# First layer's attention: full-row scores with a doubled low part of k, v split per head, and reloads issued by GpSimd

## The chip, the core and the metric

The kernel runs on one core of one Trainium2 chip. The metric is the device time of one execution in microseconds; the time given for a kernel is the median of its runs. Stretches of the profile are given in microseconds from the start of the span.

## The reference

Two layers over 1024 positions of width 1024, in float32. Layer 0 mixes with differential attention (mixer A, 4 heads) and causal pooling (mixer B); layer 1 mixes with banded attention (mixer C). Each layer ends with a gated MLP of inner width 2816 that has a width-3 causal convolution. Cut to what matters here:

```python
def diff_attention(q, k, v, lam, lam_init, sub_g):      # per head: two 64-wide maps m = 0, 1
    s = jnp.einsum('bqhmd,bkhmd->bhmqk', q, k) * scale + bias   # causal, ALiBi
    p = jax.nn.softmax(s, axis=-1)
    attn = p[:, :, 0] - lam * p[:, :, 1]
    return jnp.einsum('bhqk,bkhe->bqhe', attn, v)       # v is 128 wide per head

def conv_glu_ffn(x, norm_g, w_up, conv_w, conv_b, w_down):
    h = rms_norm(x, norm_g) @ w_up                      # 1024 -> 2 * 2816
    c = causal_conv3(h) ; gate, up = split(c)
    return x + (silu(gate) * up) @ w_down               # 2816 -> 1024
```

## The kernel before

All matrix products take float32 operands as a high and a low part (`split`: ScalarE copies the high part, VectorE or GpSimd subtracts it to get the low part; lines 125 to 128). A product of two such operands is three matmuls. The program is written with a tile framework whose scheduler orders each engine's instructions; `weave` interleaves in program order a main generator (the attention of one head) with a side generator (projections that are needed later), at a rate of side cost per main cost. Tiles come from pools of a fixed number of buffers; a new tile takes a buffer that is free, or the next one that becomes free.

The stages, by the profile: setup and pools of layer 0 (to about 100 us), projection of q, k and v of mixer A and the attention of its four heads with the output projection (about 100 to 445 us), the up half of the MLP (to about 895 us), the down half (to about 1130 us), then the same for layer 1 with mixer C.

**Scores of mixer A.** Per head, `stack_q` transposes q on TensorE and builds for each map m a tile of 128 rows: 64 rows with the high part of q, the other 64 with its low part. `stack_k` builds for each map a tile `hi` that holds the high part of k in both halves of the rows, and the low part of k. With one `lo` tile (`len(los) == 1`), map 0 has its low part in rows 0 to 63 and map 1 in rows 64 to 127 of the same tile. `scores` then issues two matmuls into one PSUM bank: line 623 over all 128 rows (q high and q low against k high), and line 624 over the 64 rows of map m (q high against k low). Mixer C calls the same functions with two `lo` tiles: line 616 copies each low part to the other 64 rows, and line 624 runs over 128 rows there.

For query block j (128 queries, j = 0 to 7) the keys come in chunks of up to 512 columns; a chunk of 128 is widened to 256. VectorE adds the bias table and takes the minimum (line 694), ScalarE exponentiates (698), VectorE combines the two maps (711), TensorE transposes the result (718), `split` (127, 128), and line 729 multiplies with v.

**v of mixer A.** `project_v` leaves v of two heads in two raw tiles (`va`, `vb`). `split_v` makes four tiles, two blocks of keys and two heads in each, once for heads 0 and 1 and once for heads 2 and 3. These tiles, q, k and others share the tag `g` with 9 buffers in this stage (`MIX_A`).

**Side work.** For heads 0 to 2 the side generator is `dense` (line 553, matmuls of 256 columns into bank `psd`); from late in head 2 it is `project_out` (line 119, into `psd`).

**The down half** (`ffn_down`). For each pair of row blocks i, `fetch` reloads the gated activations from DRAM (`gd`, into tag `gr`, 4 buffers, or `xg` for the first pair) and loads the weights (`wr`, 2 buffers); both are split. The residual x is reloaded from DRAM (line 533, 8 tiles). All these are issued by SyncE (SP), each queue in order. `contract` adds each product to x (line 268). GpSimd issues no DMA; its work is `split` subtractions (line 128) and one-column memsets (837, `claim`).

Of the kernel before, what the change touches and what calls it, by code (L numbers as in the profile page):

```python
# [14 lines left out]
F32R = mybir.dt.float32r  # L15
# [5 lines left out]
P = 128  # L21
# [43 lines left out]
class Trunk:  # L65
# [445 lines left out]
    def ffn_down(self, layer, xs, gd, after, begin=lambda: None):  # L511
        nc, I = self.nc, self.I

        def fetch(i):
            ws, gs = [], []
            for k in range(2):
                for lst, tag, stage, src in (
                        (gs, "g", "gr", gd[(i + k) * P:(i + k + 1) * P, :]),
                        (ws, "ws", "wr", I["w_down"][layer, i + k])):
                    if i == 0 and lst is gs:  # L520
                        tag = stage = "xg"
                    raw = self.big(stage)
                    nc.sync.dma_start(raw[:], src)
                    hi, lo = self.big(tag, F32R), self.big(tag, F32R)
                    with self.urgent():
                        self.split(raw[:], hi[:], lo[:])
                    lst.append((hi, lo))
            return ws, gs

        nxt = fetch(0)  # L530
        x = [self.big("x") for _ in range(ND)]
        for d in range(ND):
            nc.sync.dma_start(x[d][:], xs[d * P:(d + 1) * P, :])
        for i in range(0, NF - 2, 2):
            ws, gs = nxt
            nxt = fetch(i + 2)
            self.drain(self.contract(ws, [self.halves(g) for g in gs], x, banks="dqsdqsqs"))
        ws, gs = nxt
        begin()
        return lambda h: self.contract(ws, [self.halves(g) for g in gs], x, after, "qd", (h,))  # L540
# [107 lines left out]
                    raws[b // 4][:, (b % 4) * 256:(b % 4 + 1) * 256], po, AF.Copy, scale=r[:, b:b + 1])  # L648
            yield 2.6

    def split_v(self, raws):
        vs = []
        for i in range(4):
            v = self.big("g", F32R, (P, 2, 2, 2, P))
            src = raws[i // 2][:, (i % 2) * 512:(i % 2 + 1) * 512].rearrange("p (b h e) -> p b h e", b=2, h=2)
            for b in range(2):
                hi, lo = v[:, b, :, 0, :], v[:, b, :, 1, :]
                self.split(src[:, b], hi, lo)
            vs.append(v)
        return vs  # L660

    def a_attend(self, h, raws, vs, o, before, tails):
# [1 line left out]
        tab = self.big("t")  # L664
        nc.sync.dma_start(tab[:], I["tab_a"][h])
        q = [self.big("g", F32R) for _ in range(2)]
        k = ([self.big("g", F32R) for _ in range(2)], [self.big("g", F32R) for _ in range(1)])
        get = lambda o: (lambda b: raws[b // 4][:, (b % 4) * 256 + o:(b % 4) * 256 + o + P])
        self.stack_q(get(0), self.gq[:, 0:1], q)
        self.stack_k(get(P), self.par[:, PAR_AK:PAR_AK + 1], *k)  # L670
# [3 lines left out]
        for j in range(NB):  # L674
# [47 lines left out]
            for c, w, pt in pts:  # L722
                th, tl = self.half(F32R), self.half(F32R)
                self.split(pt[:, :w], th[:, :w], tl[:, :w])
                for kb in range(w // P):
                    b = c // P + kb
                    v = vs[b // 2][:, b % 2, h % 2].rearrange("p t e -> p (t e)")
                    for t, tt in enumerate((th, tl)):
                        nc.tensor.matmul(po[:, :256], tt[:, kb * P:(kb + 1) * P], v,  # L729
                                         start=(b == 0 and t == 0), stop=(b == j and t == 1))  # L730
# [134 lines left out]
    def layer_a(self, w, norm, bd, after):  # L865
# [55 lines left out]
                yield from self.contract(ws, [self.halves(m) for m in ms], x, banks="d")  # L921

        side, out_side = dense(), project_out()
        vs = self.split_v(va)
        mixes = [self.big("x") for _ in range(AH - 1)] + [self.big("rbc")]
        self.claim(mixes[0])
        for h in range(AH):
            if h < AH - 2:
                self.claim(mixes[h + 1])
            if h == 2:  # L930
                vs = self.split_v(vb)
            def before(h=h):
                if h > 0:
                    tails[h - 1]()
# [340 lines left out]
```

## Time and profile before

| | before |
|---|---|
| median of 3 runs | 2176.08 us (2173.35 to 2179.15) |
| profiled execution, its own time | 2179.32 us |
| its span | 2177.5 us |
| TensorE (PE) busy | 2103.5 us, 97% |
| VectorE (DVE) busy | 1648.1 us, 76% |
| ScalarE (ACT) busy | 1010.7 us, 46% |
| GpSimd (POOL) busy | 129.2 us, 6% |
| chain that ended last: share of PE | 89% |

The busy time of PE runs from a matmul's start to its modelled end, so that pipelined matmuls overlap in it: what a matmul takes from the stream is read as the distance from its start to the start of the next one.

### The profile page before, as it was taken

The page shows a single profiled execution, that of the slowest core. Times are in us where ns is not written, and L with a number is a line of the kernel's source. Part 1 is how long each engine was busy: PE and PEld are TensorE (multiplying, and loading weights), DVE is VectorE, ACT ScalarE, POOL GpSimd, SP SyncE. Part 2 cuts the span into 40 slices and gives each one's busy share as a digit, 9 for nine tenths or more (in the row PEclk, how much of TensorE's full clock was granted, in tenths as well). Part 3 has the DMA queues.
Part 4 walks back from the last instruction along what each step waited for, and adds up shares of the span by engine and source line. Part 5 has one row for each costly group of instructions (what it writes and reads, how often), then busy time and mean ns, then how long its engine had stood idle before and what let it go on. Part 6 is the DMA issues. An engine that isn't in the chain of part 4 may idle for free.

```text
span 2177.5 us, 28523 instructions
## 1 busy us (share of the span) xinstructions
PE 2103.5 (97%) x10704; PEld 1768.6 (81%) x10704; DVE 1648.1 (76%) x3015; ACT 1010.7 (46%) x1887; POOL 129.2 (6%) x88
## 2 busy tenths in 40 slices
PE   8999999989999999899999999898999999989999
PEld 7988867767888888788889998787788888878887
DVE  6676787788777878667677887787877878776665
ACT  5465555336455455312144886654645555531210
POOL 1210132000000000000002020200000000000000
PEclk9999989989999999999999999999999999999999
DMA  4210122212222122622232011221222122262222
GB/s 166 88 40 30 59 88 68 78 39 97 77 88 87 70 86 87 243 78 98 76 107 79 30 40 49 68 78 58 97 78 82 74 87 78 97 227 92 82 93 78
DMA packets 59610, 186.02 MB, mean 85 GB/s; under 512 B 6864, under 2 KB 7376, under 8 KB 59472
## 3 DMA queue, kind: packets, MB, share of 16 engines
q1 hardware_dynamic: 52560, 171.62, 22.7%
q10 hardware_dynamic: 6912, 12.59, 1.5%
q8 instruction: 84, 1.38, 0.3%
q14 instruction: 54, 0.44, 0.1%
HBM read 142.23 MB, written 41.94 MB: 85 GB/s over the span
## 4 chain that ended last, share of the span: by engine, by line
PE 89%; DVE 7%; ACT 2%; issue 1%; DMA 0%; SPq 0%; ACTq 0%; DVEq 0%
PE pss L336 22%; PE psd L119 12%; PE psq L336 12%; PE psq L119 11%; PE pss L119 8%; PE psd L553 6%; PE psd L336 5%; PE pss L553 4%; PE pss L624 2%; PE psq L729 2%; PE pss L623 1%; PE pss L778 1%; PE psq L778 1%; DVE x L305 1%; PE psq L1023 1%
## 5 line engine op out<-in xcount | busy, mean ns | idle before, releaser
L336 PE MATMUL pss<-xg,ws 128*128 128x512 f32 x1248 | 297.6, 391 | 9.1 <-DVE xg L128 5.5
L336 PEld LDWEIGHTS pss<-xg,ws 128*128 128x128 f32 x1248 | 234.9, 189 | 60.4 <-DVE xg L128 6.3
L336 PE MATMUL pss<-T,ws 128*128 128x512 f32 x912 | 225.4, 390 | 3.4 <-ACT ws L127 3.4
L119 PE MATMUL psq<-g,ws 128*128 128x512 f32 x852 | 220.0, 392 | 5.8 <-ACT g L127 3.4
L336 PEld LDWEIGHTS pss<-T,ws 128*128 128x128 f32 x912 | 171.9, 189 | 40.0 <-ACT ws L127 4.3
L119 PEld LDWEIGHTS psq<-g,ws 128*128 128x128 f32 x852 | 160.4, 189 | 39.9 <-ACT g L127 3.9
L553 PE MATMUL psd<-ws,xg 128*128 128x256 f32 x1344 | 188.9, 287 | 0.5 <-DVE hms L562 0.5
L119 PE MATMUL psd<-xg,ws 128*128 128x512 f32 x624 | 171.5, 414 | 15.2 <-DVE x L268 13.1
L127 ACT ACTIVATE ws<-wr 128x512 fp32r<-128x512 f32 (+1 forms) x176 | 145.3, 829 | 78.5 <-PE pss L119 38.3
L553 PEld LDWEIGHTS psd<-ws,xg 128*128 128x128 f32 x1344 | 170.1, 191 | 7.5 <-issue 4.1
L119 PE MATMUL pss<-g,ws 128*128 128x512 f32 x684 | 176.1, 391 | 0.0
L127 ACT ACTIVATE g<-gr 128x1024 fp32r<-128x1024 f32 x40 | 41.6, 1051 | 289.4 <-PE pss L119 289.4
L336 PE MATMUL psq<-xg,ws 128*128 128x512 f32 x696 | 169.3, 391 | 0.0
L128 DVE TENSOR_TENSOR ws<-hf,ws 128x512 fp32r<-128x512 f32 x152 | 104.0, 688 | 69.0 <-ACT ws L127 68.9
L336 PEld LDWEIGHTS psq<-xg,ws 128*128 128x128 f32 x696 | 131.4, 189 | 27.5
L268 DVE TENSOR_TENSOR x<-psq,x 128x512 f32<-128x512 f32 x160 | 109.9, 688 | 55.9 <-PE psq L119 55.5
L119 PEld LDWEIGHTS pss<-g,ws 128*128 128x128 f32 x684 | 129.4, 189 | 27.1
L119 PEld LDWEIGHTS psd<-xg,ws 128*128 128x128 f32 x624 | 116.5, 196 | 42.7 <-DVE x L268 14.9
L128 POOL TENSOR_TENSOR ws<-wr,ws 128x1024 fp32r<-128x1024 f32 x38 | 94.2, 2487 | 950.9 <-ACT ws L127 912.4
L268 DVE TENSOR_TENSOR x<-psd,x 128x512 f32<-128x512 f32 x160 | 109.9, 688 | 50.7 <-PE psd L119 48.4
L128 DVE TENSOR_TENSOR ws<-wr,ws 128x512 fp32r<-128x512 f32 (+1 forms) x138 | 119.3, 866 | 20.6 <-ACT ws L127 20.6
L119 PE MATMUL psd<-g,ws 128*128 128x512 f32 x528 | 134.0, 389 | 0.0
(212 smaller groups left out, 3791.2 us busy)
## 6 DMA issues: line engine op xcount, KB each, us to landing
wr<-in_dram SPq DMA_DIRECT2D x130, 512.0 KB, 3.7
gd<-x SPq DMA_DIRECT2D x40, 512.0 KB, 2.6
gr<-gd SPq DMA_DIRECT2D x40, 512.0 KB, 4.5
x<-in_dram SPq DMA_DIRECT2D x38, 512.0 KB, 4.4
xd<-x ACTq DMA_DIRECT2D x48, 256.0 KB, 2.3
x<-in_dram SPq DMA_DIRECT2D x32, 256.0 KB, 3.5
x<-xd SPq DMA_DIRECT2D x16, 512.0 KB, 6.0
t<-in_dram SPq DMA_DIRECT2D x10, 512.0 KB, 3.6
```

The costliest lines, as they stand in the source:

```text
L119: self.nc.tensor.matmul(out, a, b, start=(k == 0), stop=(k == n - 1))
L127: nc.scalar.activation(hi, raw, AF.Copy)
L128: (eng or nc.vector).tensor_tensor(out=lo, in0=raw, in1=hi.bitcast(F32), op=ALU.subtract)
L268: nc.vector.tensor_tensor(out=xs, in0=po[:], in1=xs, op=ALU.add)
L305: nc.vector.scalar_tensor_tensor(out=xs, in0=xs, scalar=g, in1=self.nrbc[:, sl], op0=ALU.mult, op1=ALU.mult)
L336: nc.tensor.matmul(bank[:], a, b, start=start and k == 0, stop=k == n - 1, skip_group_check=open)
L553: self.nc.tensor.matmul(out, a, m[:, d % 4, :], start=(n == 0), stop=(n == 23))
L623: nc.tensor.matmul(out, q[:, qs], his[m][:, ks], start=True, stop=False)
L624: nc.tensor.matmul(out, q[rows, qs], lo[rows, ks], start=False, stop=True)
L729: nc.tensor.matmul(po[:, :256], tt[:, kb * P:(kb + 1) * P], v, start=(b == 0 and t == 0), stop=(b == j and t == 1))
L778: nc.tensor.matmul(pu[:], a, b, start=d + n == 0, stop=d == ND - 1 and n == 2)
L1023: nc.tensor.transpose(pt[:, (2 * kb + t) * P:(2 * kb + t + 1) * P], pv[:, 2 * kv + t, k0 + kb * P:k0 + (kb + 1) * P], self.idn[:])
```

## The change

Three edits. The low part of k gets two tiles in mixer A, so that `stack_k` copies each low part to the other 64 rows (line 616, four ScalarE copies of 64x512 per head) and `scores` runs line 624 over 128 rows. `split_v` now makes the two tiles of one head, and is called at the start of each head. In the down half, the reloads of `gd` and of x are issued by GpSimd instead of SyncE; the weights stay with SyncE.

```diff
@@ ffn_down
-                    nc.sync.dma_start(raw[:], src)
+                    (nc.gpsimd if lst is gs else nc.sync).dma_start(raw[:], src)
...
-            nc.sync.dma_start(x[d][:], xs[d * P:(d + 1) * P, :])
+            nc.gpsimd.dma_start(x[d][:], xs[d * P:(d + 1) * P, :])
@@ split_v
-    def split_v(self, raws):
+    def split_v(self, raws, h):
         vs = []
-        for i in range(4):
-            v = self.big("g", F32R, (P, 2, 2, 2, P))
-            src = raws[i // 2][:, (i % 2) * 512:(i % 2 + 1) * 512].rearrange("p (b h e) -> p b h e", b=2, h=2)
-            for b in range(2):
-                hi, lo = v[:, b, :, 0, :], v[:, b, :, 1, :]
-                self.split(src[:, b], hi, lo)
+        for i in range(2):
+            v = self.big("g", F32R, (P, 4, 2, P))
+            src = raws[i][:].rearrange("p (b h e) -> p b h e", b=4, h=2)[:, :, h, :]
+            self.split(src, v[:, :, 0, :], v[:, :, 1, :])
             vs.append(v)
@@ a_attend
-        k = ([self.big("g", F32R) for _ in range(2)], [self.big("g", F32R) for _ in range(1)])
+        k = ([self.big("g", F32R) for _ in range(2)], [self.big("g", F32R) for _ in range(2)])
...
-                    v = vs[b // 2][:, b % 2, h % 2].rearrange("p t e -> p (t e)")
+                    v = vs[b // 4][:, b % 4].rearrange("p t e -> p (t e)")
@@ layer_a
-        vs = self.split_v(va)
...
-            if h == 2:
-                vs = self.split_v(vb)
+            vs = self.split_v((va, vb)[h // 2], h % 2)
```

What moves on the engines, at the two places of which the prediction speaks (lines of the changed kernel after `split_v` are two or three lower: 696 is 698 of before, 716 is 718, 727 is 729, 732 is 734).

ScalarE at the start of head 0, before: lines 609 and 610 write the high part of k, 560 and 561 evict the side work's bank, 698 exponentiates.

```order
L609 ACTIVATE g_1170<-psq_1190,par 64x512
L610 ACTIVATE g_1170<-psq_1190,par 64x512
L560 ACTIVATE x_1224<-psd_1257 128x256
L561 ACTIVATE psd_1257<-psd_1257 128x256
L609 ACTIVATE g_1169<-psq_1201,par 64x512
L610 ACTIVATE g_1169<-psq_1201,par 64x512
L698 ACTIVATE t_1316,l_1315<-t_1316,mn_1320 128x128
L609 ACTIVATE g_1170<-psq_1201,par 64x512
L610 ACTIVATE g_1170<-psq_1201,par 64x512
```

The same place in the changed kernel:

```order
L609 ACTIVATE g_1155<-psq_1190,par 64x512
L610 ACTIVATE g_1155<-psq_1190,par 64x512
L127 ACTIVATE g_2041<-x_929 128x4x128
L616 ACTIVATE g_1158<-g_1158 64x512
L560 ACTIVATE x_1215<-psd_1276 128x256
L561 ACTIVATE psd_1276<-psd_1276 128x256
L616 ACTIVATE g_1157<-g_1157 64x512
L609 ACTIVATE g_1156<-psq_1190,par 64x512
L610 ACTIVATE g_1156<-psq_1190,par 64x512
L696 ACTIVATE t_1307,l_1306<-t_1307,mn_1311 128x128
```

The copies of the low part (616) stand between the high parts and the evictions of the side work, and the first half of head 1's v (`g_2041`) is split already here.

SyncE at the head of layer 0's down half, before (`wr` weights, `gr` and `xg` gated activations, `x` the residual, 357 a store of the up half):

```order
L357 DMA gd_72<-x_8081 128x1024
L523 DMA wr_8407<-in_dram 128x1024
L523 DMA gr_8249<-gd_72 128x1024
L533 DMA x_8233<-xd_69 128x1024
L533 DMA x_8234<-xd_69 128x1024
L533 DMA x_8235<-xd_69 128x1024
L533 DMA x_8236<-xd_69 128x1024
L523 DMA gr_8261<-gd_72 128x1024
L523 DMA gr_8401<-gd_72 128x1024
L523 DMA gr_8413<-gd_72 128x1024
L523 DMA wr_8419<-in_dram 128x1024
L533 DMA x_8237<-xd_69 128x1024
```

GpSimd at that place in the changed kernel:

```order
L523 DMA gr_8253<-gd_72 128x1024
L533 DMA x_8237<-xd_69 128x1024
L533 DMA x_8238<-xd_69 128x1024
L533 DMA x_8239<-xd_69 128x1024
L533 DMA x_8240<-xd_69 128x1024
L523 DMA gr_8265<-gd_72 128x1024
L523 DMA gr_8405<-gd_72 128x1024
L523 DMA gr_8417<-gd_72 128x1024
L533 DMA x_8241<-xd_69 128x1024
L533 DMA x_8242<-xd_69 128x1024
L523 DMA gr_8557<-gd_72 128x1024
L533 DMA x_8243<-xd_69 128x1024
```

The reloads keep their order among themselves and leave the weights' queue; they stand alone on GpSimd, the eighth tile of x as the sixteenth of the row that begins with `gr_8253`.

## Rows read from the trace of the kernel before

**Rows 1.** The page, part 1: engine, busy us, share, instructions.

```profile
PE 2103.5 (97%) x10704; PEld 1768.6 (81%) x10704; DVE 1648.1 (76%) x3015; ACT 1010.7 (46%) x1887; POOL 129.2 (6%) x88
```

**Rows 2.** Windows: stretch and length; busy us of PE, PEld, DVE, ACT, POOL; clock; DMA.

```profile
260.00:300.00 40.00, 37.86 (x179) 27.11 (x177) 34.28 (x95) 29.59 (x69) 18.00 (x12) 0.83 0.36 119
360.00:380.00 20.00, 19.20 (x85) 12.61 (x84) 18.15 (x48) 12.15 (x30) 10.35 (x5) 1.00 0.42 132
140.00:450.00 310.00, 297.01 (x1685) 239.40 (x1685) 242.08 (x649) 160.68 (x367) 47.78 (x30) 0.97 0.20 65
```

**Rows 3.** Chain in order of time (start, us, what): matmuls of 512 columns.

```profile
540.52 2.72 PE pss L336 x12
```

**Rows 4.** Timeline of PE, two places in mixer A (start, us, engine, line, operation).

```profile
165.72 0.39 PE L623 MATMUL pss<-g,g 128*128 128x512 f32 x1
166.04 0.49 PE L624 MATMUL pss<-g,g 64*128 64x512 f32 x1
166.46 0.50 PE L623 MATMUL pss<-g,g 128*128 128x512 f32 x1
166.89 0.50 PE L624 MATMUL pss<-g,g 64*128 64x512 f32 x1
167.32 0.86 PE L553 MATMUL psd<-ws,xg 128*128 128x256 f32 x5
...
210.34 0.36 PE L623 MATMUL pss<-g,g 128*128 128x256 f32 x1
210.63 0.38 PE L624 MATMUL pss<-g,g 64*128 64x256 f32 x1
210.94 0.74 PE L553 MATMUL psd<-ws,xg 128*128 128x256 f32 x4
```

**Rows 5.** Timeline of PE in mixer C, where line 624 has 128 rows.

```profile
1207.49 0.28 PE L624 MATMUL pss<-g,g 128*128 128x256 f32 x1
1207.60 0.28 PE L623 MATMUL pss<-g,g 128*128 128x256 f32 x1
1207.72 0.28 PE L624 MATMUL pss<-g,g 128*128 128x256 f32 x1
```

**Rows 6.** Groups by line and form: count, busy us, mean ns, idle before.

```profile
L624 PE MATMUL pss<-g,g 64*128 64x512 f32 x48 | 24.6, 512 | 0.0
L624 PE MATMUL pss<-g,g 64*128 64x256 f32 x32 | 11.9, 381 | 2.3 <-DVE g L612 2.3
L624 PE MATMUL pss<-g,g 64*128 64x384 f32 x16 | 7.0, 438 | 0.0
```

**Rows 7.** Windows of line 624 alone: PE and PEld busy us (and count).

```profile
260.00:300.00 40.00, 8.91 (x18) 3.70 (x18) 0.83 0.36 119
360.00:380.00 20.00, 5.26 (x13) 2.19 (x12) 1.00 0.42 132
```

**Rows 8.** Line 616 in mixer C: ns min/median/max, first and last start, form.

```profile
L616 ACT ACTIVATE g<-g x4: 617/631/635, 1195.8 to 1203.2; 64x512 fp32r<-64x512 f32 x4
```

**Rows 9.** Timeline of GpSimd and VectorE at 190 us.

```profile
190.35 2.39 POOL L128 TENSOR_TENSOR ws<-wr,ws 128x1024 fp32r<-128x1024 f32 x1
190.50 2.26 DVE L165 TENSOR_TENSOR nt<-nt,zh 128x4 f32<-128x4 f32 x1
```

**Rows 10.** Timeline at the head of layer 0's down half: SyncE, VectorE, PE.

```profile
890.28 2.68 SPq L533 DMA_DIRECT2D x<-xd  x4
...
904.38 0.69 DVE L268 TENSOR_TENSOR x<-psd,x 128x512 f32<-128x512 f32 x1
...
905.12 2.93 PE L119 MATMUL psd<-xg,ws 128*128 128x512 f32 x6 [5.71 <-DVE x L268]
...
925.30 1.29 DVE L268 TENSOR_TENSOR x<-psq,x 128x512 f32<-128x512 f32 x2 [0.66 <-PE psq L119]
```

**Rows 11.** The page, part 6: count, KB each, us from issue to landing.

```profile
x<-xd SPq DMA_DIRECT2D x16, 512.0 KB, 6.0
```

**Rows 12.** Windows: the loop of layer 0's down half.

```profile
950.00:1100.00 150.00, 150.00 (x663) 124.24 (x662) 103.89 (x138) 27.36 (x28) 0.00 (x0) 1.00 0.25 81
```

## The prediction, on record before the run

> **What bounds the kernel now.** I read the page first: PE is busy for 97% of the span and is most of the chain that ended last [rows 1]. So time goes only where PE's stream gets shorter, or where PE waits. Then the windows: over mixer A's attention, 140 to 450 us, PE is busy 297.0 of 310 us, DVE 242.1, ACT 160.7 [rows 2]. Two stretches in it are unlike the rest: at 260 to 300 and at 360 to 380 us DVE is busy 34.3 of 40 and 18.2 of 20 us and PE is not full. Outside them DVE is busy 242.1 - 34.3 - 18.2 = 189.6 of 250 us, 76%, and PE has next to no gaps. There the PE stream is the bound; in the two stretches the chain through DVE is. Last the timeline of PE, by starts: a busy time overlaps the next one, a start does not.
>
> **Scores: what a 64-row matmul takes from the stream.** A matmul of 512 columns in a plain run starts every 2.72/12 = 0.227 us [rows 3]; one of 256 columns, full rows, every 0.11 to 0.12 us, and this holds for lines 623 and 624 themselves in mixer C [rows 5]. In mixer A the same pair is far slower [rows 4]: from 165.72 the starts are 0.32 and 0.42 us apart, then 0.43 and 0.43, so a pair of 512 takes 0.74 to 0.86 us, 0.80 in the mean, where two plain ones take 0.45; the pair of 256 takes 0.29 + 0.31 = 0.60 where 0.24 would do. So each change between 128 and 64 rows costs some 0.1 to 0.2 us, on the matmul ahead of it and on the 64-row one. The excess is 0.35 us at 512, 0.36 at 256, and I take 0.36 at 384. With the counts [rows 6] that is 48 x 0.35 + 32 x 0.36 + 16 x 0.36 = 34 us of PE's stream. All of it goes, since the changed kernel has mixer C's form here. If the short kind of pair (0.74) were the rule, it would be 48 x 0.29 + 48 x 0.36 = 31.
>
> The Trainium skill (TensorE: Matmul & The Clock Gate, section "Why this matters for your kernels") points the other way: a single matmul on few rows takes as long as one on 128, and a gain comes only from several running at once. By that rule the 64-row matmul was never dear and the change gives PE nothing. The trace disagrees for matmuls in a mixed stream: 0.42 us against 0.227.
>
> **How much of the 34 us shortens the run.** Of the 96 pairs 18 + 13 = 31 lie in the two stretches that DVE bounds [rows 7], 11 us of the excess; 65 lie where PE bounds, 23 us. Where PE bounds, DVE goes from 189.6 of 250 to 189.6 of 227 us, 84%, so it does not become the bound on the whole, but PE's order is fixed, and an attention matmul that comes sooner finds its DVE result less often ready. The gain there lies between 23 and, if half is lost to such waits, 11 us; I take three quarters, 17, since DVE still has room. In the two stretches it lies between 11 and 0; I take a quarter, 3, nearer to 0, since PE there waits anyway. The clock was granted at 0.83 in the first of them, so part of that stretch ran at the lower level; I count nothing for it.
>
> **What the scores edit adds.** Sixteen ScalarE copies (line 616) at 0.63 us [rows 8], 10 us on an engine that is half idle: nothing by themselves. But they lengthen the way to a head's first scores by one or two copies, 0.6 to 1.3 us, and ScalarE waits in them for DVE's subtraction (line 612); queued behind them are the evictions 560 and 561, for which the side matmuls wait. In the changed order some 24 side matmuls stand between the first line 623 and line 624 of head 0 (none before) and 22 in head 1 (4 before): 24 x 0.12 = 2.9 us of cover. Bare, four heads would pay 2.4 to 5.2 us; covered, nothing; I take 1. By the same order the attention falls back against its side work by up to some 25 matmuls in heads 0 to 2, so the side work ends sooner against the heads that follow; I take 2 us for that, between 0 and 25 x 0.12 = 3.
>
> **v per head.** Half as many splits over the same elements: no gain counted. A head holds 8 of the 9 `g` buffers, and the second low tile of k of the next head takes the buffer of the last head's first v tile, so it waits for that head's last product. Between a head's last scores and the next head's first stand some 140 side matmuls in the first case, before and after, 17 us: nothing. Without that cover it would be one more chain of transposes and copies at three boundaries.
>
> **Reloads by GpSimd.** Sixty issues leave SyncE. In the loop PE is busy 150.00 of 150 us [rows 12], so a sooner or later reload changes nothing there. Only the heads of the two passes have something to win or lose: PE idles 5.71 us before 905.12, released by a DVE add at 904.38 [rows 10]. The x tiles for it were issued from 890.28 and land 6.0 us later in the median [rows 11], at 896.3, 8.1 us ahead of the add. So the add waited its turn on DVE, behind convolutions, and moving the loads cannot bring it forward. The order on DVE stays but for one gate product (1.2 us) ahead of four adds; between 0 and 1.2 us a pass, and I take 0, since PE drains a bank in 6 x 0.227 = 1.36 us and DVE adds in 0.6. No row shows a DMA issued by GpSimd. Its time on GpSimd is bounded by SyncE's 2.68/4 = 0.67 us [rows 10] and by GpSimd's own pass over 128x1024, 2.39 us [rows 9]; I take a value near the lower, as an issue does not walk the elements. Sixteen reloads from `gr_8253` to the eighth x tile pass in order; that tile is wanted at 925.30, so there is no loss up to (925.3 - 6.0 - 890.3)/16 = 1.8 us each. I take 0.
>
> **Sum.** -17 - 3 + 1 + 2 + 0 = -17 us. The profiled run, 2179.3 us (its span 2177.5 and 1.8 around it), would become 2162; it lies 3.2 us above the median of 2176.1, to which the same step gives 2159.
>
> **The rivals.** *All of it counts:* the 34 us go and DVE keeps pace. For it speaks that DVE's 242 us fit into 276; against it the two stretches near DVE's limit. 2176 - 34 + 0 to 3 = 2142 to 2145.
>
> *DVE takes over:* the waits grow by what PE saves. For it speaks that DVE is over 85% busy in 60 of the 310 us, and that GpSimd holds it up: a four-column operation took 2.26 us while GpSimd ran its pass at 190.35 [rows 9]. Against it, the 76% elsewhere. Loss of three quarters of the 23 us and of all the 11, with 3 paid: 2176 - 6 + 3 = 2173, so 2169 to 2177. Here belongs also that full rows bring nothing, because the slow pairs were waiting for something else: 2176 + 1 to 3 = 2177 to 2179, at 0.03; the rows speak against it, since plain and mixed pairs differ in a stream that waits for nothing. This is what the page cited above would have.
>
> *The reloads come late:* each reload holds GpSimd longer than 1.8 us, its queue is in order, and at the head of each down pass the DVE adds, with PE behind them, wait for the last x tiles. At 2.39 us the eighth tile lands (16 x 2.39) - (16 x 1.8) = 9 us late, 19 in two passes, and cancels the gain: 2178. At 3 us it is 16 x 1.2 = 19 a pass: 2159 + 38 = 2197. It decides from about 2.5 us. For it speaks that GpSimd and DVE hold each other up [rows 9] and that DVE is packed at that place; against it that a plain issue on SyncE takes a third.
>
> The Trainium skill (SBUF — State Buffer, section "SBUF: two separate sides") warns of this: a DMA that GpSimd issues has its descriptors written by GpSimd, which is locked out while DVE runs an operation that uses both ports for one tensor. No run here shows it so far; the operations of DVE in the down half take two tensors, so I leave the chance low.
>
> **How the numbers follow.** The forecast, 2151 to 2167: 0.58. All of it counts: 0.13. DVE takes over, full rows for nothing included: 0.18. Late reloads, 2170 to 2200: 0.11. For 8 in 10 the range takes the forecast, the upper part of the first rival and most of the second: 2144 to 2175. About 0.3%, 6.5 us, is what a measurement of this kernel can tell from no change: faster is below 2169.6, slower above 2182.6. Faster: 0.58 + 0.13 + 0.05 of the second rival + 0.01 of the third = 0.77; slower: 0.07 of the third; the same: 0.16.
>
> **What would show it.** In the profile after: starts 0.227 apart at lines 623 and 624 with 512 columns and 0.12 with 256; 140 to 450 us shorter by some 17 us, with DVE's share up and PE's waits on line 694's and 128's results up; idle time of PE at the heads of the down passes again near 5.7 us; GpSimd's issues under 1.8 us. It is wrong if the attention ends no sooner though the starts are close (DVE took over), if the starts stay apart (the rows were not the cause), or if PE's idle time before line 119 grows.

## The result, and the profile after

The changed kernel takes 2164.69 us in the median of 4 runs (2162.63 to 2166.92), the kernel before 2177.61 us in the runs beside them: a ratio of 0.9944, 95% interval 0.9931 to 0.9958, so by this ratio 12.2 us or 0.56% faster (the medians lie 12.9 us apart). The forecast was 2159 with a range of 2144 to 2175. The sign, the place and the mechanism of the gain were right; the gain is 12 us where 17 were forecast, and two errors of opposite sign stand behind that small difference. Of all the executions of the runs below one, of e6_zero_first, took 3455.18 us at a mean granted clock of 0.556; its ratio leaves it out.

In the page's part 1 of the changed kernel, PE is 31 us less busy than in [rows 1], ScalarE 8 us more (the copies), GpSimd 32 us more (the reloads' issues):

```profile
PE 2072.1 (96%) x10704; PEld 1768.5 (82%) x10704; DVE 1644.9 (76%) x3007; ACT 1019.0 (47%) x1895; POOL 161.0 (7%) x148
```

The pairs of the scores have the plain distance now. Timeline of PE in mixer A (start, us, engine, line, operation), to be held against [rows 4]:

```profile
206.34 0.39 PE L623 MATMUL pss<-g,g 128*128 128x512 f32 x1
206.57 0.40 PE L624 MATMUL pss<-g,g 128*128 128x512 f32 x1
206.81 2.18 PE L553 MATMUL psd<-ws,xg 128*128 128x256 f32 x17
...
211.39 0.28 PE L623 MATMUL pss<-g,g 128*128 128x256 f32 x1
211.51 0.28 PE L624 MATMUL pss<-g,g 128*128 128x256 f32 x1
211.63 0.64 PE L553 MATMUL psd<-ws,xg 128*128 128x256 f32 x4
```

From 206.34 the starts are 0.23 and 0.24 us apart, where 0.32 to 0.43 stood before; at 256 columns 0.12 and 0.12, as in mixer C [rows 5]. The last product with v starts at 414.6 us instead of 427.6, the first matmul of the MLP at 433.8 instead of 445.8, 12.0 us sooner. (The two profiled executions lie 15.9 us apart. Most of the 4 us behind the attention fall in layer 1's MLP: from mixer C's last scores to the last matmul of line 336 it is 566.1 us before and 563.4 after, where kernels with the same order of work lie between 560 and 567.) What was not kept shows in the windows (columns as in [rows 2]) and in PE's waits:

```profile
260.00:300.00 40.00, 29.88 (x134) 23.64 (x133) 34.66 (x94) 27.16 (x66) 17.63 (x12) 0.83 0.33 106
140.00:450.00 310.00, 282.42 (x1721) 248.74 (x1719) 246.37 (x658) 172.32 (x382) 47.68 (x30) 0.96 0.21 67
```

From 260 to 300 us PE is busy 29.9 of 40 us, where it was 37.9 [rows 2]. PE's waits from 100 us to the end of the attention (line waited at, releaser: us in total, times, longest), first of the kernel before:

```profile
PE psq L119 <- DVE x L268: 3.0, 1, 3.0
PE pss L624 <- DVE g L612: 2.3, 1, 2.3
PE psq L729 <- DVE hf L128: 1.7, 3, 0.8
PE pss L623 <- DVE mn L694: 1.7, 3, 1.1
```

The same view of the changed kernel:

```profile
PE pss L624 <- ACT g L616: 6.4, 3, 4.3
PE pss L623 <- DVE mn L692: 4.9, 5, 2.3
PE psq L119 <- DVE x L268: 2.6, 1, 2.6
PE psq L727 <- ACT hf L127: 2.3, 2, 1.4
PE psd L553 <- DVE hms L562: 1.8, 3, 0.8
PE pss L623 <- ACT g L610: 1.8, 2, 1.0
```

The largest new wait is for line 616, the copies of the low part that the change adds. Of the 6.4 us, 5.9 lie at the head of head 2. Timeline of PE there, with its waits:

```profile
258.30 0.38 PE L624 MATMUL pss<-g,g 128*128 128x256 f32 x1 [1.52 <-ACT g L616]
259.70 0.51 PE L623 MATMUL pss<-g,g 128*128 128x256 f32 x2 [1.02 <-ACT g L610]
...
264.77 0.79 PE L624 MATMUL pss<-g,g 128*128 128x256 f32 x2 [4.33 <-ACT g L616]
```

**Where the 12 us come from, by head.** Take the time from each matmul's start to the next one's, from 100 us to the first matmul of the MLP. Of it, count as work the plain distance (0.227 us at 512 columns, 0.172 at 384, 0.120 at 256, 0.109 for a transpose; what stood there, where that is less); as change of rows up to 0.1 us for each neighbour with another number of rows; as lower clock what the work takes more where the granted clock was at its lower level; the rest is waiting. In us:

| | length | work | changes of rows | lower clock | waits |
|---|---|---|---|---|---|
| head 0, before / after | 82.6 / 76.4 | 72.0 / 72.5 | 9.4 / 0 | 0 / 0 | 1.2 / 3.9 |
| head 1 | 77.5 / 72.0 | 64.3 / 66.1 | 9.0 / 0 | 0 / 0 | 4.3 / 5.9 |
| head 2 | 77.8 / 77.9 | 58.5 / 56.3 | 9.4 / 0 | 4.9 / 4.4 | 5.0 / 17.3 |
| head 3 | 89.8 / 88.4 | 75.2 / 75.3 | 9.0 / 0 | 0 / 3.8 | 5.6 / 9.4 |
| the tail | 18.1 / 19.1 | 9.5 / 9.5 | 0 / 0 | 1.6 / 1.6 | 7.0 / 8.0 |
| sum | 345.8 / 333.8 | 279.5 / 279.6 | 36.7 / 0 | 6.5 / 9.8 | 23.0 / 44.4 |

(A head's row ends with its last product with v, line 729: at 182.5, 260.0, 337.8 and 427.6 us before, at 176.2, 248.2, 326.2 and 414.6 after.) Heads 0 and 1 save 18.4 us of row changes and are 11.7 us shorter; the rest went into waits (4.3) and into side work that moved there (2.3). Head 2 saves 9.4 and waits 12.3 more; head 3 keeps 1.4.

**The reloads.** Groups by line on GpSimd (count, busy us, mean ns), and the head of layer 0's down half on PE:

```profile
L523 POOL DMA_DIRECT2D gr<-gd x40 | 21.2, 530 | 336.7 <-DVE g L128 276.2 <-PE pss L336 60.5
L533 POOL DMA_DIRECT2D x<-xd x16 | 8.5, 530 | 29.6 <-DMA gd<-x 16.5 <-issue 6.7 <-DVE x L356 4.6
```

```profile
892.37 2.93 PE L119 MATMUL psd<-xg,ws 128*128 128x512 f32 x6 [5.71 <-DVE x L268]
```

An issue holds GpSimd 0.53 us, and PE idles 5.71 us as in [rows 10], to the hundredth.

### The profile page after: what moved, and what is told of

It reads as the page before. It is cut to its first block, busy times and chain, and to the rows that moved or that the text cites. A ratio compares the mean times of both kernels' runs of the same rounds, so it can differ in the third digit from the quotient of the medians.

```text
span 2161.4 us, 28559 instructions
## 1 busy us (share of the span) xinstructions
PE 2072.1 (96%) x10704; PEld 1768.5 (82%) x10704; DVE 1644.9 (76%) x3007; ACT 1019.0 (47%) x1895; POOL 161.0 (7%) x148
## 4 chain that ended last, share of the span: by engine, by line
PE 87%; DVE 8%; ACT 4%; issue 1%; DMA 0%; SPq 0%; ACTq 0%; DVEq 0%
PE pss L336 22%; PE psq L336 12%; PE psd L119 12%; PE psq L119 11%; PE pss L119 8%; PE psd L553 5%; PE psd L336 5%; PE pss L553 4%; PE psq L727 1%; PE pss L776 1%; PE psq L776 1%; DVE x L305 1%; PE pss L623 1%; PE pss L624 1%; PE psq L1020 1%
## 5 line engine op out<-in xcount | busy, mean ns | idle before, releaser
L127 ACT ACTIVATE ws<-wr 128x512 fp32r<-128x512 f32 (+1 forms) x176 | 145.1, 829 | 75.6 <-PE pss L119 36.7
L268 DVE TENSOR_TENSOR x<-psq,x 128x512 f32<-128x512 f32 x160 | 109.7, 688 | 56.3 <-PE psq L119 55.8
L119 PEld LDWEIGHTS psd<-xg,ws 128*128 128x128 f32 x624 | 117.3, 196 | 38.4 <-DVE x L268 14.2
L344 DVE SCALAR_TENSOR_TENSOR x<-x,conv,x 128x1023 f32<-128x1023 f32 x80 | 102.3, 1281 | 30.5 <-ACT x L343 30.5
```

The costliest lines, as they stand in the source:

```text
L119: self.nc.tensor.matmul(out, a, b, start=(k == 0), stop=(k == n - 1))
L127: nc.scalar.activation(hi, raw, AF.Copy)
L268: nc.vector.tensor_tensor(out=xs, in0=po[:], in1=xs, op=ALU.add)
L344: nc.vector.scalar_tensor_tensor(out=c[:, 1:], in0=hr[:, :S - 1], scalar=cw(1), in1=c[:, 1:], op0=ALU.mult, op1=ALU.add)
```

## The experiments

Each run was compared with the kernel before on the same chip (2176.2 to 2176.7 us). "End" is the first matmul of layer 0's MLP in the profiled execution, against 445.8 us in the kernel before; it separates the attention, where all edits but the reloads lie, from what comes later. Each end is read in one execution; the executions of e11_pool_v lie 12 us apart in their whole time, and the one read is the longest of the six (2190.76 us), that of e7_grouped the shortest of its eight.

| run | median us | ratio (95%) | end |
|---|---|---|---|
| changed kernel | 2164.69 | 0.9944 (0.9931 to 0.9958) | -12.0 |
| e1_scores_v | 2167.21 | 0.9956 (0.9943 to 0.9968) | -11.3 |
| e2_reloads | 2175.13 | 0.9999 (0.9990 to 1.0008) | +0.6 |
| e3_half_rows | 2187.29 | 1.0047 (1.0034 to 1.0060) | +11.2 |
| e4_zero | 2165.35 | 0.9950 (0.9936 to 0.9963) | -18.1 |
| e5_v_only | 2197.04 | 1.0088 (1.0073 to 1.0104) | +13.9 |
| e6_zero_first | 2153.88 | 0.9894 (0.9879 to 0.9909) | -21.9 |
| e7_grouped | 2184.30 | 1.0025 (1.0015 to 1.0036) | +2.8 |
| e8_dve_before | 2205.34 | 1.0136 (1.0121 to 1.0152) | +23.6 |
| e9_dve_after | 2170.14 | 0.9975 (0.9965 to 0.9985) | -1.0 |
| e10_pool_before | 2176.85 | 1.0006 (0.9994 to 1.0019) | +4.9 |
| e11_pool_v | 2185.33 | 1.0036 (1.0019 to 1.0052) | +5.5 |
| e12_pool_after | 2150.17 | 0.9879 (0.9864 to 0.9893) | -24.5 |

### The reloads: with the rest, and alone

```diff
# e1_scores_v, against the changed kernel
-                    (nc.gpsimd if lst is gs else nc.sync).dma_start(raw[:], src)
+                    nc.sync.dma_start(raw[:], src)
-            nc.gpsimd.dma_start(x[d][:], xs[d * P:(d + 1) * P, :])
+            nc.sync.dma_start(x[d][:], xs[d * P:(d + 1) * P, :])
```

> The changed kernel with its reloads given back to SyncE; full rows, two low tiles and v per head stay. My theory: all of the gain is made in the attention of layer 0 (its last product with v starts 13.0 us sooner in the changed kernel), the reloads give nothing, so this is 12 to 14 us faster than the kernel before and within 2 us of the changed kernel's 2164.7, and PE idles 5.71 us at the head of both down passes. Rival: the reloads on GpSimd bring some 3 us (the profiled spans differ by 16.2 us, 3 more than at the end of layer 0's MLP): then this is 9 to 10 us faster only, and the second MLP is some 3 us longer than in the changed kernel.

The kernel before with only these two lines as in the change is e2_reloads:

> The kernel before with the 60 reloads issued by GpSimd and nothing else. My theory: each issue holds GpSimd 0.53 us, as in the changed kernel's trace, far below the 1.8 us that the queue has free, and the adds at the heads of the down passes wait their turn on VectorE: 0, at most 1.5 us either way, PE idle 5.71 us at both heads. Rival: the reloads bring some 3 us, by which the profiled span is shorter than the attention explains: 2174.

Without the reloads on GpSimd the rest of the change gives 0.9956, 9.6 us. That is not the 12 to 14 us that were expected but the size that the rival named, and as the rival had it, layer 1 is longer: from mixer C's last scores to the last matmul of line 336 it takes 566.9 us, against 563.4 in the changed kernel. But the reloads don't show as the cause. Alone on GpSimd they give 0.9999, between 2.2 us faster and 1.7 us slower, so a gain of 3 us is outside the interval (the rival's 2174, a ratio of 0.9990, is its edge). And where the reloads lie, the kernels don't differ. From the end of the attention to mixer C's last scores, which holds all of layer 0's, the seven kernels here with reloads by SyncE take 920.5 to 923.3 us (median 921.8), the seven with reloads by GpSimd 920.4 to 923.4 (921.2); from the last matmul of line 336 to the end of the span, which holds most of layer 1's, 243.0 to 244.2 (243.5) and 243.2 to 244.5 (243.8). In the stretch that is 3.5 us longer in e1_scores_v the granted clock was at its lower level, half of the higher, for 27.3 us, in the changed kernel for 17.1. PE idles 5.71 us at the heads of both down passes in both runs.

### The full rows: undone alone

```diff
# e3_half_rows, against the changed kernel (mixer A only)
-        rows = slice(0, P) if len(los) > 1 else slice(m * 64, (m + 1) * 64)
+        rows = slice(m * 64, (m + 1) * 64)
```

> The changed kernel, with its copies, its two low tiles, v per head and reloads by GpSimd, but line 624 over the 64 rows of its map again in mixer A. My theory: the change between 128 and 64 rows is what was dear; the starts after lines 623 and 624 go back to 0.32 to 0.43 us at 512 columns, 32 us of PE's stream return, and as PE's waits shrink again by some 12 to 20 us, the time is back at that of the kernel before or up to 4 us above it (the copies): 2175 to 2182. Rival (rows cost nothing, the gain came from the new order of the side work, or from v): it keeps at least half of the 13 us, 2170 or less.

The rows are the gain: with 64 rows, and everything else of the change in place, the kernel is 10 us slower than the kernel before and 22.6 us slower than the changed one. Timeline of PE, with the old distances of 0.41 and 0.42 us:

```profile
142.00 0.48 PE L623 MATMUL pss<-g,g 128*128 128x512 f32 x1
142.41 0.49 PE L624 MATMUL pss<-g,g 64*128 64x512 f32 x1
142.83 0.86 PE L553 MATMUL psd<-ws,xg 128*128 128x256 f32 x5
```

By the table's counting, changes of rows are 35.8 us here, waits 30.0 (44.4 in the changed kernel), lower clock 11.2 (9.8): of 35.8 us the full rows keep 23. By head the changed kernel is 10.0, 6.8, -0.2 and 7.0 us shorter than this one. The edit undoes one thing more than the rows: line 624 does not read the copied rows here, and PE waits for no line 616. So the 23 us are what the full rows bring less what waiting for the copies costs. But the time was expected up to 4 us above the kernel before, and it is 10: the copies' time on ScalarE, v and the new order together cost 11.2 us at the end of the attention, where the prediction had 3.

### v per head, alone

```diff
# e5_v_only, against the kernel before
+    def split_v(self, raws, h):      # two tiles of one head, as in the change
-        vs = self.split_v(va)
-            if h == 2:
-                vs = self.split_v(vb)
+            vs = self.split_v((va, vb)[h // 2], h % 2)
```

> The kernel before with v split per head and nothing else (one low tile, 64-row matmuls, reloads on SyncE). The run with 64 rows showed that the changed kernel without its full rows is some 10 us slower than the kernel before; this asks how much of it is v per head. My theory: the copies of the low part and the waits behind them are most of it; v per head is the same elements in half as many splits, moved to each head's start: 0 to 3 us slower, 2176 to 2179. Rival: the split at each head's start, and the order of side work that follows from it, are the cost: 5 to 10 us slower, 2181 to 2186, with PE waiting for ScalarE at the starts of heads 1 and 3, where the kernel before splits no v.

My theory falls, and the rival's size falls too: 19 us slower, 13.9 of them in the attention. Nor is the place the rival's: head 1 ends 0.8 us sooner than before, head 2 is 9.3 us longer and head 3 6.1, and PE does not wait for ScalarE at the starts of heads 1 and 3. In head 2 waits are 10.9 us (5.0 before) and lower clock 8.6 (4.9); the granted clock of a stretch that holds the first blocks of head 2, from the windows, first of the kernel before and then of this one:

```profile
252.90:328.80 75.90, 73.76 (x380) 56.78 (x379) 62.14 (x166) 42.25 (x99) 22.03 (x15) 0.91 0.24 77
```

```profile
250.50:336.00 85.50, 78.99 (x393) 60.16 (x392) 66.34 (x169) 44.40 (x103) 21.78 (x15) 0.84 0.23 76
```

A mean of 0.84 over 85.5 us is some 27 us at the lower level, half of the higher (0.16 x 2 x 85.5), against 14 before. The clock fell at 275.1 us, behind waits of 0.3 and 0.6 us, and rose again at 288.8; between the two PE waited 1.3 and 2.4 us. What it waited for is seen on VectorE, GpSimd and PE there:

```profile
275.98 1.20 DVE L573 TENSOR_TENSOR hz<-hz,r 128x32 f32<-128x32 f32 x1
...
278.30 1.30 DVE L705 SCALAR_TENSOR_TENSOR al<-l,neglam,rl 128x1 f32<-128x1 f32 x1
279.53 1.29 DVE L702 SCALAR_TENSOR_TENSOR oe<-l 128x1 f32<-128x1 f32 x1
280.75 1.43 DVE L709 SCALAR_TENSOR_TENSOR t<-t,al,t 128x128 f32<-128x128 f32 x1
```

```profile
277.08 4.94 POOL L128 TENSOR_TENSOR xg<-wr,xg 128x512 fp32r<-128x512 f32 x4
```

```profile
282.23 0.47 PE L716 MATMUL psq<-idn,t 128*128 128x128 f32 x1 [2.36 <-DVE t L709]
```

Operations on one column take 1.3 us, as long as one of GpSimd's four passes beside them (4.94/4 = 1.24). They stand in the chain from the scores to the transposes, and PE waits at its end.

### Without GpSimd's passes

To test whether those passes are the cause, three kernels leave them out in all of layer 0's attention (28 passes in the kernel before, the first at 108 us, where the expectation below has 25); the high part stands in for the low part. They are the kernel before, the one with v per head alone, and the changed kernel, each with this edit.

```diff
# e10_pool_before, e11_pool_v, e12_pool_after
-        with self.urgent():
-            self.split(raw[:], hi[:], lo[:], eng or nc.gpsimd)
-        return hi, lo
+        with self.urgent():
+            nc.scalar.activation(hi[:], raw[:], AF.Copy)
+        return hi, hi
# and in split_mix
-            self.split(m[:, sl], hi[:, sl], lo[:, sl], self.nc.gpsimd)
-        return hi, lo
+            nc.scalar.activation(hi[:, sl], m[:, sl], AF.Copy)
+        return hi, hi
```

> The kernel before without GpSimd's subtractions for the mixes and weights that are split from the middle of layer 0's attention on (25 passes of 1.3 and 2.4 us; the high part stands in for the low part in the products, PE's work is the same). In the trace of the kernel before, every VectorE operation of the attention that took over 0.1 us more than others of its kind ran beside such a pass, 26 us in sum. This is the base for the two runs that go with it; expected 4 to 10 us faster than the kernel before by itself, the operations of VectorE with one column all at 0.15 to 0.25 us.

> The same edit on the kernel with v per head alone, which was 14 us later than the kernel before at the end of the attention (waits 6.5 us more, TensorE's lower clock 8 us more, nearly all in heads 2 and 3). Theory A: v per head moves the first steps of heads 2 and 3 onto GpSimd's passes, VectorE's short operations take 1.2 to 1.4 us there, PE waits, and the clock falls: without the passes the attention ends within 4 us of the run e10_pool_before. Theory B (the order of the engines alone, GpSimd has no part in it): the 14 us stay, 10 or more.

> The same edit on the changed kernel. If what PE waits for in heads 2 and 3 comes from GpSimd's passes (theory A), the attention is 18 to 28 us sooner than in e10_pool_before, not the 12.0 us between the kernels with the passes; if it comes from the order of work on ScalarE and VectorE (theory B), the difference stays at 10 to 15 us.

Between the three, theory A holds: v per head ends the attention 0.6 us later than its base (5.5 against 4.9), not 13.9, and the changed kernel 29.4 us sooner (-24.5 against 4.9), not 12.0 and a little more than the 18 to 28 that were expected. (In the total e11_pool_v is 8.5 us behind its base; it has the dearer order of layer 1 of which the next section speaks.) A rival is that PE itself waited for the subtractions that are gone: from 100 us to the end of the attention it waits for no result of GpSimd in any of the three kernels that have them. From 251 to 332 us e11_pool_v has a clock of 0.96, and the one-column operations of VectorE, lines 705 and 702 above, take 0.16 to 0.22 us in the mean:

```profile
251.00:332.00 81.00, 79.29 (x430) 63.52 (x429) 56.24 (x170) 48.28 (x107) 0.00 (x0) 0.96 0.34 105
```

```profile
L709 DVE SCALAR_TENSOR_TENSOR al<-l,neglam,rl 128x1 f32<-128x1 f32 x8 | 1.7, 215 | 0.1
L706 DVE SCALAR_TENSOR_TENSOR oe<-l 128x1 f32<-128x1 f32 x8 | 1.2, 155 | 1.2 <-ACT t L700 1.2
```

But the base itself missed its forecast: e10_pool_before is not faster than the kernel before (1.0006; its attention ends 4.9 us later), though VectorE's long operations are gone. The scheduler lays out each of these kernels anew, and this order must be a worse one somewhere else, which no run shows. Nor is it the sum of the delays that counts: from 100 us to the end of the attention, the operations of VectorE that took over 0.1 us more than the median of their kind lost 23.1 us in the kernel before (18 of them), 27.2 in e5_v_only (21) and 20.7 in the changed kernel (18); each of them ran beside a pass, and without the passes there is none. That it is a question of where they fall is argued, not shown. So the passes explain why the same edits cost more or less, and the size of it within some 5 us; they don't explain each kernel's time, and which of the moved instructions of e5_v_only lost the most was not taken apart.

### The copies: zeros in their place

The other 64 rows of a low tile need not hold a copy: with zeros there, line 624 computes what the kernel before does. GpSimd writes them, since that waits for no result, only for the buffer.

```diff
# e4_zero, against the changed kernel, in stack_k for mixer A
-                    nc.scalar.activation(lo[other, sl], lo[rows, sl].bitcast(F32), AF.Copy)
+                    nc.gpsimd.memset(lo[other, sl].bitcast(F32), 0.0)
```

> The changed kernel with the 16 ScalarE copies of the low part replaced by GpSimd writing zeros in the same 64 rows (the product of the two low parts, which the copies add, is left out, as in the kernel before). My theory: the copies are what was mis-sized: in the changed kernel PE idles 6.4 us for line 616 and 1.8 us for line 610 behind it, where I had counted 1 us. The zeros wait for nothing but the buffer and leave ScalarE 10 us, so 4 to 8 us of this come back: 2157 to 2161. Rival (VectorE is the bound there, and takes over when ScalarE is free): under 2 us, the waits for lines 692 and 709 grow by what those for 616 lose. A second rival: GpSimd's passes over 64 rows hold up VectorE's short operations (2.26 us instead of 0.16 at 190.50 in the kernel before) and eat the gain.

The total says nothing gained (2165.35 against 2164.69), and would have buried the theory; the stages say otherwise. The attention ends 6.1 us sooner than in the changed kernel, within what was expected, and stays ahead through mixer C; then layer 1's MLP loses it. The second rival has no part in it: 12 operations of VectorE ran beside these passes and beside nothing else of GpSimd, and none took more than 0.01 us over the median of its kind. In layer 1 the scheduler put 71 matmuls of line 336, not 34, ahead of the transposes of that MLP's norm, and PE has to wait for the norm's end:

```profile
1492.96 0.50 PE L336 MATMUL pss<-xg,ws 128*128 128x512 f32 x1 [2.13 <-ACT xg L127]
1498.74 1.65 PE L336 MATMUL pss<-xg,ws 128*128 128x512 f32 x3 [4.59 <-DVE xg L128]
```

From the last scores of mixer C to the last matmul of line 336 the nine kernels with 34 (the two of the comparison among them) take 560.3 to 566.9 us, 563.4 in the median, the five with 71 take 565.3 to 572.4, 569.1 in the median. The two ranges touch, but the 5.7 us between the medians go with the order, and it falls on edits that have nothing to do with layer 1: e5_v_only, e7_grouped, e8_dve_before and e11_pool_v have it too.

The next kernel keeps the idea and has the order with 34:

```diff
# e6_zero_first, against the changed kernel, in stack_k for mixer A
+        for m, lo in enumerate(los):
+            nc.gpsimd.memset(lo[(1 - m) * 64:(2 - m) * 64, :].bitcast(F32), 0.0)
...
-                    nc.scalar.activation(lo[other, sl], lo[rows, sl].bitcast(F32), AF.Copy)
```

> The changed kernel with zeros instead of the copies of the low part, as in the run e4_zero, but one pass of GpSimd over 64 x 1024 for each tile, ahead of the transposes of k, not four passes of 64 x 512 among them (8 in the attention, not 16). In e4_zero the attention ended 6.1 us sooner than in the changed kernel, but 7.6 us were lost in layer 1, where the scheduler put 71 matmuls of the MLP ahead of the transposes of its norm (line 236), not 34, and PE then waited 2.1 and 4.6 us for x; here the order of that place is that of the changed kernel. My theory: the attention ends some 6 us sooner than in the changed kernel and layer 1 gives nothing back: 2157 to 2161. Rival (what is saved at the heads' starts is lost again wherever it falls, since VectorE or a later stage bounds the whole): 2163 to 2167.

It is faster than both kernels: 2153.88 us, 0.9894 (0.9879 to 0.9909), 10.8 us below the changed kernel and better than the theory had it. The attention ends 9.9 us sooner than in the changed kernel: 7.5 less of waits and 3.2 less of lower clock. The eight passes cost GpSimd 0.95 us each, and PE waits for no line 616; the longest waits that are left are for VectorE's results:

```profile
L604 POOL MEMSET g<- 64x1024 f32 x8 | 7.6, 948 | 3.0 <-PE pss L626 2.6
```

```profile
PE pss L626 <- DVE mn L695: 4.1, 6, 1.9
PE psq L730 <- DVE hf L128: 3.2, 2, 2.5
PE psq L719 <- DVE t L712: 2.8, 2, 1.5
PE pss L627 <- DVE oR L171: 2.6, 1, 2.6
```

### How near VectorE is to being the bound

```diff
# e8_dve_before (kernel before), e9_dve_after (changed kernel)
-            nc.vector.tensor_reduce(
-                ob, po[:, :256].rearrange("p (t e) -> p e t", t=2), axis=AX.X, op=ALU.add)
+            for _ in range(3):
+                nc.vector.tensor_reduce(
+                    ob, po[:, :256].rearrange("p (t e) -> p e t", t=2), axis=AX.X, op=ALU.add)
```

> The kernel before with VectorE's sum of the two halves of the product with v done three times instead of once: 64 more passes of 128x256 at 0.41 us, 26 us more of VectorE in the attention of layer 0, nothing else. With the same edit on the changed kernel it asks how near VectorE is to being the bound there. My theory: outside the two stretches VectorE has room, so a part only is paid: 6 to 12 us slower than the kernel before. Rival (VectorE already bounds): 20 us or more.

> The changed kernel with the same 64 extra passes of VectorE (26 us). My theory: PE's stream is shorter there by 32 us, so VectorE's work shows more: 9 to 17 us slower than the changed kernel, a few us more than the same edit costs in the kernel before; that part is what VectorE took of the gain. Rival (VectorE has taken over): 22 to 26 us, all of it. Other rival (VectorE has nothing to do with what was lost): no more than in the kernel before.

Only the size in the changed kernel's attention was as expected; the comparison was not. The 26 us of VectorE cost the kernel before 23.6 us at the end of the attention (29 in the total, where the order with 71 adds to it), which is the size of the rival, and the changed kernel 11.0 (7 in the total). So VectorE's added work costs less, not more, after the change: "VectorE takes over" is not what ate the gain. In waits and lower clock together the kernel before loses nothing in heads 0 and 1, 8.3 us in head 2 and 17.3 in head 3; the changed kernel loses 14.2 in head 3 and nothing in head 2, where it already waited for ScalarE. So VectorE has room in the first two heads and none in the last, in both kernels. Because these two also have an order of their own, the two prices are not the same thing measured twice.

### What is dear about 64 rows

```diff
# e7_grouped, against the kernel before
-                    self.scores(s[:, :e], m, q[m], k, slice(j * P, (j + 1) * P), slice(c, c + e))
+                for c, w, e, s in cs:
+                    nc.tensor.matmul(s[:, :e], q[m][:, qs], his[m][:, c:c + e], start=True, stop=False)
+                for c, w, e, s in cs:
+                    nc.tensor.matmul(s[:, :e], q[m][rows, qs], lo[rows, c:c + e], start=False, stop=True)
```

> The kernel before with the scores of blocks 4 to 7 in another order: for each map first line 623 of both chunks, then line 624 of both, where the banks allow. It asks what is dear, each change between 128 and 64 rows, or each 64-row matmul. If the change: a 64-row matmul behind another one starts the next at the plain 0.23 (512 columns) or 0.12 us (256), and a block saves two changes of 0.1 to 0.2 us for each map, 32 pairs of chunks in all, so up to 10 us of PE's stream, less waits. If every 64-row matmul is slow by itself, the starts after it stay at 0.42 and 0.31 us and the time is that of the kernel before.

In the order that came out, two 64-row matmuls stand in a row at 8 places only (2 in the kernel before), of 32 possible. Timeline of PE at one with 512 columns in both:

```profile
164.52 0.64 PE L695 MATMUL pss<-g,g 128*128 128x512 f32 x2
165.08 0.73 PE L697 MATMUL pss<-g,g 64*128 64x512 f32 x2
165.74 1.33 PE L553 MATMUL psd<-ws,xg 128*128 128x256 f32 x9
```

The two of line 695 take 0.56 us (0.23 and 0.33), the two of line 697 0.66 (0.34 and 0.32). Four alternating ones took 0.32, 0.42, 0.43 and 0.43 [rows 4], 1.60 in sum; these take 1.22. So it is the change: each costs about 0.1 us on the matmul ahead of it and 0.1 us on the one behind, whichever of the two has 64 rows, and a 64-row matmul with no change beside it would by this sum take the plain 0.23 (no run has three in a row). The Trainium skill (TensorEngine Tiling (Array Packing), section "Key Properties") says that changing the tiling mode drains the engine; the trace agrees, if a change of row count is such a change, with 0.2 us. The kernel itself is 0.25% slower, not faster: 36.7 us of changes became 34.2, and the lower clock and the waits grew by 3.1 and 1.8 us.

## Why the prediction came out as it did

**The bound and the price of 64 rows: right.** PE's stream was the bound, and the pairs have the plain starts that were forecast. The excess was put at 34 us, from two kinds of pair; counted over every matmul it was 36.7, as the matmul behind a pair pays 0.1 us too. The rival that full rows bring nothing, and the page of the Trainium skill behind it, fall with e3_half_rows, though not the page's sentence itself: by e7_grouped it is the mixing with 128 rows that is dear, and no run has 64-row matmuls by themselves.

**How much of it counts: right.** Three quarters where PE bounds and a quarter where VectorE does gave 20 of 34. Undone alone, the full rows are worth 22.6 us in the total and 23 at the end of the attention, and the split by place is right in kind: against e3_half_rows, of some 9 us a head, 10.0 and 6.8 us are kept in heads 0 and 1, 7.0 in head 3 and none in head 2. That head 2 gives nothing is in part luck: VectorE was named as the bound there, and of PE's waits in head 2 of the changed kernel 4.8 us are for VectorE's results, but 6.9 for the copies and line 610.

**What the scores edit adds: the first step that failed.** One microsecond was taken for 16 copies, because 22 to 24 side matmuls stand between the first line 623 and line 624. That cover was read in heads 0 and 1 and taken for all four. Head 2 has none: PE waited 1.52, 1.02 and 4.33 us there. Zeros written by GpSimd instead gave 9.9 us back. The prediction's own bound for copies without cover, 2.4 to 5.2 us in four heads, was too low as well: it priced a copy at its length, not at the queue of an engine that works without a gap, as ScalarE did there (busy 14.3 of the 14.7 us from 253.0 to 267.7).

**v per head: the second, and the largest.** It was counted at nothing, by the number of elements. Alone it costs 13.9 us in the attention. The term that was missing is the one named for the drift of the order, put at 2 us between 0 and 3: the edit gives heads 2 and 3 another order, and beside GpSimd's passes that order costs 13.9 us, without them 0.6. The rows for these passes stood in the prediction [rows 9] and were used for the rivals only, not for the price of an order. The sum of what the change adds was forecast at 3 us and is 11.2, PE's waits for the copies not counted.

**The clock: a term left out.** "I count nothing for it" stood beside the stretch at 0.83. In the attention, the lower level cost 6.5 us before and 9.8 after, 14.7 in e5_v_only. What brought it on stays open: it does not follow the sum of PE's waits (47.3 us of waits and 7.5 of lower clock in e1_scores_v, 30.0 and 11.2 in e3_half_rows).

**The reloads: right,** in time (0.9999), in mechanism (0.53 us an issue, between no and the 1.8 us that were free) and in the idle time of 5.71 us at the heads of the down passes. No run shows GpSimd's issues held up by VectorE.

**The rivals.** *DVE takes over* is not what happened: VectorE's share from 140 to 450 us rose only from 78 to 79%, the gain is in the forecast's band, and extra work of VectorE costs the changed kernel less than the kernel before. *All of it counts* did not happen here; e12_pool_after against its base, 29 of 36 us, comes nearest and shows what stands in the way. The forecast was 5 us off because the full rows gave 3 us more and the rest cost 8 more; that it was no more than 5 is luck, since the two errors have opposite signs.

## What to carry to other kernels

Look at the starts of matmuls, not at their busy times, wherever matmuls on 64 and 128 rows alternate in a stream that waits for nothing: filling the other rows with zeros, written by an idle engine ahead of time, takes the changes away and waits for nothing but the buffer. When an edit adds a step to a chain, look for its cover at every place where it stands, above all where the engine that runs it has no gap; and where a scheduler orders the engines, measure by stage, since an edit can win its own stage and lose the total in one that it doesn't touch.

## What the runs showed of the hardware

- A change of a matmul's row count between 128 and 64 costs about 0.2 us, half on each side of it.
- VectorE operations on a few columns last as long as GpSimd's subtraction beside them: one-column operations 1.29 and 1.30 us in e5_v_only, 0.16 to 0.22 where the passes are left out. In the kernel before, from 100 us to the end of the attention, every operation of VectorE that took over 0.1 us more than others of its kind overlapped such a pass, 18 operations and 23 us in sum. The Trainium skill (SBUF — State Buffer, section "Who interferes with whom") states this: VectorE and GpSimd share a pair of ports under an exclusive lock, and a VectorE instruction with two inputs in SBUF contends with a GpSimd instruction that reads SBUF. The trace agrees, with 1.24 us for a pass and 1.30 for the operation.
- GpSimd's writing of zeros does not hold VectorE up: of 12 operations of VectorE beside such passes alone in e4_zero, and 17 in e6_zero_first, none took more than 0.07 us over the median of its kind.
- A reload of 512 KB issued by GpSimd takes 0.53 us of it. From issue to landing the x tiles take 6.6 us in the median, against 6.0 from SyncE [rows 11], the `gr` tiles 3.7 against 4.5.
